# A two-layer diffusion transformer on one core: five of seven written-out instruction orders are replaced by orders from another search

## The chip, the cores and the metric

The kernel runs on one core of a Trainium2 chip. The metric is the time on the device, in microseconds (us), of one execution. The engines are TensorE (PE in the rows; PEld is its weight load), VectorE (DVE), ScalarE (ACT) and GpSimd (POOL); transfers between memory and the chip's SBUF are DMAs, most of them issued by SyncE (SP). Each engine works through its own queue in order.

## The reference, cut to what matters

The input is 512 latent tokens and 256 context tokens of width 1024, in float32. Layer 0 mixes tokens in two ways, by a long convolution ("Hyena") and by attention with 8 heads over 2 key heads, and layer 1 by a chunked matrix memory (mLSTM) in both directions. Around each mixer stand an adaptive norm, an output product, a second norm and a residual:

```python
        h_lat = rms_norm(x_lat, g_pre[layer]) * (1 + sc_l[:, None]) + sh_l[:, None]
        ...
            y_lat, y_ctx = even_mixer(h_lat, h_ctx, rows, cols, need_ctx, e_w_in[j], ...
            y_lat, y_ctx = odd_mixer(h_lat, h_ctx, need_ctx, o_w_in[j], ...
        x_lat = x_lat + ga_l[:, None] * rms_norm(y_lat, g_post[layer])
```

So between the layers each tile of 128 tokens goes through a chain: product with the output weights, norm of the product, gate, residual, norm for layer 1, scale and shift, and only then into the products of layer 1. After layer 1 only the 512 latent tokens are wanted.

## The kernel before

Every float32 product is made from values split in a high and a low part, by three matmuls (`mm3`, line 1015): high by high, high by low, low by high. Weights come in as `wr` by DMA, ScalarE copies the high part (`wh`) and VectorE subtracts to get the low part (`wl`); activations are split in the same way (`hTh`, `hTl`).

The program falls into seven regions, which follow each other: `start` (the norms and first products), `hy` (the long convolution), `att` (attention), `out0` (output product of layer 0, the norms between the layers and the first products of layer 1), `l1a` (layer 1's projections), `l1b` (its recurrence over 12 chunks of 64 tokens) and `out1` (its output product, norm and residual). In each region the code does not issue its operations at once. `record` (line 990) opens a list, every call on an engine is appended to it, and `play` (line 995) issues the whole list in the order of `ORDERS[name]`, a list of numbers: number i is the i-th operation that was recorded. All operations of a region are issued at line 1000, so all rows carry that line, and the names of the tiles tell operations apart. `tc.keep_in_program_order(x)` (line 1003) holds each engine's queue to that order. What an operation waits for across engines (data, a buffer that has to come free) is found from its operands and is not part of the order:

```python
        for i in ORDERS.get(name) or range(len(work)):
            e, fn, a, k = work[i].work
            x = fn(*a, **k)
```

A second table, `SLOTS`, says which of a tile's buffers the n-th allocation of a tag takes (`T`, line 930): "xn@9" is the tag `xn` in the tenth pool. A buffer is written again only when all readers of its previous tile are done. PSUM tiles are `pj` and `pm`, four buffers each in `out0`, `l1a` and `l1b`.

In `out0` the six tiles of tokens (4 and 5 are the context) go through these steps (`out_stages` from line 2074, `epi0`): the last product of the tile on PE (12 matmuls of 512 columns), `add` to `yacc` on VectorE, squares on ScalarE, reduce to `ess` and `esst` on VectorE, the power -1/2 `ers` on GpSimd (`rstd`, line 1076: one column of 128 values), the weighing by the gate `gg`, two multiply-adds into `xt` (residual), squares on ScalarE, `sst` on VectorE, the power `rs` on GpSimd, two `xn` on VectorE, eight transposes of `xn` on PE into `pm`, `hf` (scale and shift, shared by VectorE and ScalarE) and the split into `hTh` and `hTl`. Products of tiles that are ready with layer 1's first weights (288 columns) stand at the end of the region.

Of the kernel before, what the change touches and what calls it, by code (L numbers as in the profile page):

```python
# [151 lines left out]
class Ctx:  # L152
# [586 lines left out]
        0, 1, 2, 3, 4, 5,  # L739
    ],  # L740
    "sst@0": [
        0, 1, 4, 2, 3, 5,
    ],
    "rs@0": [
        0, 1, 2, 3, 4, 5,
# [150 lines left out]
        0, 1, 0, 1,  # L896
    ],
    "xt@15": [
        2, 0, 1, 3,
    ],  # L900
}

# [1875 lines left out]
```

## Time and profile before

| what | us |
|---|---|
| profiled execution, its time | 1491.61 |
| its span, from the first to the last instruction | 1489.8 |
| runs shown | 1490.02, 1491.35, 2872.85 |
| median of them | 1491.35 |
| PE busy in the span | 1457.7 (98%) |

The 1.8 us between span and time lie around the profiled instructions. The regions follow each other on PE with hardly an overlap; their borders by PE's first matmul are 0, 51.0, 423.6, 741.7, 878.4, 1043.9 and 1396.2 us, and the last matmul starts at 1481.44 us. TensorE's granted clock is given as a share of 2.4 GHz; its mean here is 0.997.

### The profile page before, as it was taken

The numbers are of one execution on the slowest core, as the hardware profiler recorded it, in microseconds if no ns is written. First come the engines' busy times: TensorE is split into PE (matmuls) and PEld (weight loads), VectorE is DVE, ScalarE is ACT, GpSimd is POOL, SyncE is SP. The second block draws the span as 40 slices with busy tenths as digits, with TensorE's granted clock in tenths as the row PEclk, the third lists the DMA queues.
The fourth block names the chain that finished last, engine by engine and source line by source line (L and its number), as shares of the span: only waits on it lengthen the run. The fifth ranks groups of instructions, "written<-read, shape, count | busy, mean of one in ns | idle before, by whom it ended". The sixth has DMA issues, their size and how long they took to land. (4 is left out here: it accounts for less than half of the span.)

```text
span 1489.8 us, 25927 instructions
## 1 busy us (share of the span) xinstructions
PE 1457.7 (98%) x10362; PEld 1339.3 (90%) x10362; DVE 1037.1 (70%) x1927; ACT 766.3 (51%) x1577; POOL 82.5 (6%) x125
## 2 busy tenths in 40 slices
PE   7999999999999999999999989999999999999997
PEld 5889999989998998989997789999999999999986
DVE  6687777887865666668325888666777777877455
ACT  6634343434435444446332567645766676666442
POOL 1100000001010000000000100000100000100000
PEclk9999999999999999999999999999999999999999
DMA  9755565457331121233462334675433322324463
GB/s 378 221 140 144 146 162 131 147 140 183 76 100 43 54 96 54 82 117 114 164 222 68 134 123 155 203 267 198 156 117 97 113 62 86 124 88 140 153 205 123
DMA packets 57353, 205.79 MB, mean 138 GB/s; under 512 B 7003, under 2 KB 8539, under 8 KB 54448
## 3 DMA queue, kind: packets, MB, share of 16 engines
q1 hardware_dynamic: 50968, 181.85, 35.9%
q0 software_dynamic: 5392, 21.11, 7.4%
q8 instruction: 81, 1.33, 0.4%
q10 hardware_dynamic: 872, 1.18, 0.3%
q14 instruction: 40, 0.33, 0.1%
HBM read 182.06 MB, written 51.41 MB: 157 GB/s over the span
## 5 line engine op out<-in xcount | busy, mean ns | idle before, releaser
L1000 PE MATMUL pj<-wh,hTh 128*128 128x256 f32 (+2 forms) x1200 | 340.6, 290 | 0.8 <-ACT qjunk L1000 0.4
L1000 PE MATMUL pj<-wl,hTh 128*128 128x256 f32 (+2 forms) x1200 | 337.4, 287 | 0.3 <-DVE wl L1000 0.3
L1000 PE MATMUL pj<-wh,hTl 128*128 128x256 f32 (+2 forms) x1200 | 336.7, 288 | 0.0
L1000 PE MATMUL pj<-hTh,wh 128*128 128x512 f32 (+1 forms) x832 | 286.8, 346 | 0.4 <-DVE vl L1000 0.3
L1000 PE MATMUL pj<-hTl,wh 128*128 128x512 f32 (+1 forms) x832 | 285.4, 344 | 0.4 <-DVE hTl L1000 0.4
L1000 PE MATMUL pj<-hTh,wl 128*128 128x512 f32 (+1 forms) x832 | 285.5, 345 | 0.0
L1000 PEld LDWEIGHTS pj<-wh,hTh 128*128 128x128 f32 x1200 | 224.3, 189 | 6.2 <-issue 2.7
L1000 PEld LDWEIGHTS pj<-wl,hTh 128*128 128x128 f32 x1200 | 225.0, 189 | 2.9 <-DVE wl L1000 0.5
L1000 PEld LDWEIGHTS pj<-wh,hTl 128*128 128x128 f32 x1200 | 223.9, 189 | 3.5 <-issue 1.5
L1000 DVE TENSOR_TENSOR wl<-wr,wh 128x1024 fp32r<-128x1024 f32 (+1 forms) x142 | 171.4, 1213 | 63.9 <-ACT wh L1000 63.9
L1000 ACT CAST wh<-wr 128x1024 fp32r<-128x1024 f32 (+1 forms) x142 | 146.7, 1043 | 83.4 <-PE pj L1000 55.8
L1000 PEld LDWEIGHTS pj<-hTh,wh 128*128 128x128 f32 x832 | 156.6, 189 | 18.5 <-DVE vl L1000 1.1
L1000 PEld LDWEIGHTS pj<-hTl,wh 128*128 128x128 f32 x832 | 156.8, 189 | 17.9 <-DVE hTl L1000 0.7
L1000 PEld LDWEIGHTS pj<-hTh,wl 128*128 128x128 f32 x832 | 156.4, 188 | 18.0 <-DVE wl L1000 0.3
L1000 DVE TENSOR_TENSOR PTl<-pj,PTh 128x384 fp32r<-128x384 f32 (+1 forms) x80 | 41.1, 526 | 18.8 <-ACT PTh L1000 18.4
L1000 ACT CAST PTh<-pj 128x384 fp32r<-128x384 f32 (+1 forms) x80 | 35.6, 459 | 30.5 <-PE pj L1000 29.8
L1000 DVE TENSOR_TENSOR wl<-ch,wh 128x1024 fp32r<-128x1024 f32 x28 | 34.2, 1221 | 24.5 <-ACT wh L1000 24.4
L1000 DVE TENSOR_REDUCE mx<-s 128x1 f32<-128x768 f32 (+1 forms) x48 | 37.2, 775 | 11.4 <-PE s L1000 11.2
L1000 PE MATMUL pm<-Rh,dfa 128*128 128x256 f32 (+1 forms) x192 | 45.0, 305 | 0.0
L1000 DVE TENSOR_TENSOR med<-big 128x512 f32<-128x512 f32 (+1 forms) x48 | 40.4, 864 | 5.0 <-ACT big L1000 4.8
L1000 PE MATMUL s<-dfa,qTh 128*128 128x256 f32 (+1 forms) x160 | 42.8, 338 | 0.7 <-ACT hdh L1000 0.6
L1000 DVE SCALAR_TENSOR_TENSOR C<-C,apb,pj 128x258 f32<-128x258 f32 x64 | 30.8, 481 | 16.5 <-PE pj L1000 11.8
(374 smaller groups left out, 3172.1 us busy)
## 6 DMA issues: line engine op xcount, KB each, us to landing
wr<-in_e_w_in SPq DMA_DIRECT2D x52, 512.0 KB, 5.3
wr<-in_o_w_in SPq DMA_DIRECT2D x50, 512.0 KB, 5.2
o_sums<-in_o_w_in POOLq DMA_DIRECT2D x28, 512.0 KB, 7.1
ch<-o_sums SPq DMA_DIRECT2D x21, 512.0 KB, 4.9
wh<-in_w_mod SPq DMA_DIRECT2D x10, 1024.0 KB, 7.3
wl<-in_w_mod SPq DMA_DIRECT2D x9, 1024.0 KB, 7.6
wr<-in_e_w_out SPq DMA_DIRECT2D x16, 512.0 KB, 4.5
wr<-in_o_w_out SPq DMA_DIRECT2D x16, 512.0 KB, 4.6
```

What stands on the lines that cost most here:

```text
L1000: x = fn(*a, **k)
```

## The change

The body of the program is the same, and no instruction is added or removed. Replaced are the lists of numbers in `ORDERS` for `att`, `out0`, `l1a`, `l1b` and `out1` (those for `start` and `hy` stay), and the buffer numbers in `SLOTS` that go with them. The operations of `start` and `hy` keep their buffers, some under another number. An operation's place in the list moves by 26 (att), 32 (out0), 11 (l1a), 22 (l1b) and 32 (out1) places on the mean, by some hundreds at most. The orders come from a search that works with assumed durations, here with longer ones for GpSimd's small operations and for landings of transfers; neither the search nor its durations are part of the program.

The core of the diff, where the last tiles of `out0` go through their norms, and two of the buffer tables:

```diff
@@ -304,514 +304,514 @@
...
-        665, 666, 664, 663, 667, 682, 643, 670, 671, 672, 676, 675, 674, 677, 683, 684, 644, 646, 645, 685, 756, 686, 687, 688, 689, 668, 690, 691,
-        728, 729, 730, 692, 731, 708, 709, 678, 718, 719, 720, 721, 725, 710, 711, 712, 713, 714, 715, 716, 717, 738, 735, 694, 724, 722, 695, 693,
-        739, 740, 732, 741, 742, 743, 744, 745, 746, 747, 748, 749, 734, 733, 696, 765, 766, 767, 699, 698, 723, 726, 727, 750, 768, 769, 770, 771,
-        772, 736, 701, 702, 751, 737, 773, 774, 753, 754, 775, 703, 705, 787, 788, 704, 791, 752, 792, 755, 757, 777, 778, 776, 779, 782, 780, 929,
-        783, 784, 781, 758, 789, 790, 785, 794, 700, 815, 760, 793, 786, 761, 797, 798, 799, 800, 801, 802, 803, 804, 805, 806, 807, 808, 824, 825,
-        826, 827, 828, 829, 830, 831, 832, 795, 833, 834, 835, 856, 762, 809, 857, 858, 859, 860, 861, 862, 863, 796, 810, 763, 812, 927, 836, 837,
-        838, 839, 924, 813, 932, 764, 811, 814, 817, 816, 864, 865, 928, 866, 867, 843, 846, 819, 842, 840, 820, 821, 868, 847, 848, 849, 925, 956,
-        822, 883, 933, 957, 884, 885, 934, 935, 936, 937, 938, 852, 759, 823, 869, 871, 930, 872, 980, 886, 981, 873, 853, 841, 870, 844, 874, 875,
-        876, 818, 850, 851, 854, 931, 845, 878, 879, 855, 890, 939, 940, 880, 889, 888, 882, 958, 959, 960, 961, 893, 894, 895, 896, 962, 963, 964,
-        965, 966, 967, 898, 900, 968, 969, 887, 970, 971, 972, 973, 897, 941, 942, 943, 944, 945, 946, 913, 947, 899, 948, 914, 915, 949, 974, 975,
-        976, 881, 903, 904, 905, 877, 891, 892, 982, 901, 906, 902, 983, 984, 985, 986, 987, 988, 909, 916, 918, 907, 910, 917, 919, 950, 951, 952,
...
+        665, 643, 666, 681, 682, 683, 684, 685, 686, 687, 688, 663, 689, 690, 691, 671, 672, 676, 697, 674, 706, 692, 707, 708, 709, 710, 711, 644,
+        646, 712, 713, 714, 715, 716, 717, 738, 739, 740, 694, 695, 667, 696, 675, 645, 673, 677, 693, 699, 698, 701, 728, 729, 730, 731, 678, 741,
+        668, 742, 743, 744, 732, 734, 735, 733, 745, 746, 747, 748, 749, 750, 702, 751, 718, 719, 720, 723, 765, 724, 721, 766, 767, 722, 725, 726,
+        768, 769, 770, 771, 772, 773, 774, 775, 776, 797, 798, 736, 703, 799, 800, 753, 801, 754, 752, 756, 923, 700, 705, 824, 704, 815, 755, 757,
+        758, 760, 802, 803, 804, 787, 727, 759, 788, 789, 737, 777, 793, 761, 762, 781, 790, 778, 779, 780, 783, 784, 791, 805, 806, 807, 794, 808,
+        825, 826, 827, 828, 829, 830, 782, 831, 832, 833, 834, 835, 809, 792, 785, 763, 836, 837, 810, 786, 812, 813, 764, 795, 796, 811, 841, 846,
+        847, 848, 814, 816, 849, 817, 927, 924, 850, 852, 928, 856, 857, 858, 859, 860, 861, 862, 863, 864, 865, 819, 820, 866, 956, 867, 840, 868,
+        930, 853, 838, 839, 842, 925, 957, 958, 843, 821, 823, 893, 932, 869, 871, 872, 931, 822, 873, 844, 874, 875, 851, 870, 876, 854, 845, 878,
+        855, 879, 959, 894, 895, 960, 961, 933, 934, 935, 962, 963, 964, 965, 966, 896, 899, 898, 897, 900, 883, 967, 968, 969, 970, 884, 885, 886,
+        889, 890, 901, 936, 937, 980, 981, 877, 887, 971, 972, 938, 888, 973, 974, 939, 940, 941, 942, 943, 891, 880, 881, 882, 902, 944, 945, 946,
+        892, 903, 904, 905, 906, 910, 908, 913, 907, 917, 914, 909, 915, 916, 947, 920, 948, 949, 950, 951, 918, 975, 976, 919, 952, 953, 954, 982,
...
     "yraw@9": [
-        1, 1, 0, 0, 0, 1, 1, 1,
+        1, 1, 1, 0, 0, 1, 0, 1,
     ],
...
     "xn@9": [
-        1, 0, 1, 2, 2, 0, 1, 2, 0, 1, 0, 2,
+        1, 0, 1, 2, 2, 0, 1, 0, 0, 2, 1, 2,
     ],
...
```

Numbers of `out0` that matter here: the last matmul of the last product is 690 for tile 0, 749 for tile 1, 808 for tile 2, 867 for tile 3. The transposes are 718 to 721 and 728 to 731 (tile 5), 777 to 780 and 787 to 790 (tile 0), 836 to 839 and 846 to 849 (tile 1), 883 to 886 and 893 to 896 (tile 2), 903 to 906 and 913 to 916 (tile 3). On VectorE 809 and 868 are the `add` of tiles 2 and 3, 812, 813 and 871, 872 the reduces and `esst`, 811 and 870 the weighing, 816, 817 and 875, 876 the multiply-adds, 820 and 879 `sst`, 822, 823 and 881, 882 the `xn`; 763 and 764 are the `xn` of tile 1; 925, 928 and 931 are the low parts `wl` of layer 1's first weights. On GpSimd 703, 762, 821 and 880 are the powers `rs` of tiles 0 to 3, 814 and 873 the powers `ers` of tiles 2 and 3.

## Rows read from the trace of the kernel before

**Rows 1.** The page: busy us and share of the span, by engine.

```profile
PE 1457.7 (98%) x10362; PEld 1339.3 (90%) x10362; DVE 1037.1 (70%) x1927; ACT 766.3 (51%) x1577; POOL 82.5 (6%) x125
```

**Rows 2.** Windows by region: us; PE, PEld, DVE, ACT, POOL busy; PEclk; DMA; GB/s.

```profile
0.00:423.60 423.60, 412.69 (x2696) 368.93 (x2697) 327.47 (x542) 190.53 (x306) 32.07 (x52) 1.00 0.59 166
423.60:741.70 318.10, 314.14 (x2414) 292.10 (x2412) 201.59 (x480) 148.12 (x383) 14.37 (x9) 1.00 0.27 93
741.70:878.40 136.70, 130.57 (x794) 111.33 (x794) 81.43 (x143) 60.63 (x116) 8.94 (x15) 0.99 0.42 144
878.40:1043.90 165.50, 164.79 (x1321) 161.98 (x1322) 120.37 (x160) 100.70 (x138) 0.00 (x0) 1.00 0.58 192
1043.90:1396.20 352.30, 349.86 (x2596) 331.91 (x2595) 265.29 (x546) 238.10 (x584) 24.90 (x45) 1.00 0.33 106
1396.20:1489.80 93.60, 85.64 (x550) 73.06 (x548) 40.91 (x59) 28.27 (x53) 2.22 (x4) 0.98 0.52 182
```

**Rows 3.** PE's waits in att, first of seven lines: us in total, times, longest.

```profile
PE pj L1000 <- ACT qjunk L1000: 0.9, 3, 0.4
...
```

**Rows 4.** PE's waits in out0, all of them.

```profile
PE pm L1000 <- DVE xn L1000: 4.0, 5, 1.0
PE pm L1000 <- ACT hf L1000: 0.6, 1, 0.6
PE pj L1000 <- DVE wl L1000: 0.3, 1, 0.3
```

**Rows 5.** PE's waits in l1a, all of them.

```profile
PE pm L1000 <- DVE wa L1000: 1.3, 1, 1.3
PE pj L1000 <- DVE cvo L1000: 0.7, 1, 0.7
```

**Rows 6.** PE's waits in l1b, all of them; out1 has none.

```profile
PE pj L1000 <- DVE vl L1000: 2.1, 4, 1.1
PE pm L1000 <- DVE hh L1000: 0.2, 1, 0.2
```

**Rows 7.** Tile rs on GpSimd: shortest, median, longest ns; first and last start.

```profile
L1000 POOL TENSOR_TENSOR rs<-sst,mhalf x12: 549/562/1074, 5.8 to 863.4; 128x1 f32<-128x1 f32 x12
```

**Rows 8.** PE's timeline, tile 0 of out0: start, us, [idle before, releaser].

```profile
835.01 0.40 PE L1000 MATMUL pj<-wl,yoh 128*128 128x512 f32 x1
835.24 0.40 PE L1000 MATMUL pj<-wh,yol 128*128 128x512 f32 x1
835.90 0.66 PE L1000 MATMUL pm<-c_ident,xn 128*128 128x128 f32 x4 [0.27 <-DVE xn L1000]
...
845.56 0.81 PE L1000 MATMUL pm<-c_ident,xn 128*128 128x128 f32 x4 [0.90 <-DVE xn L1000]
```

**Rows 9.** Windows, tiles 2 and 3 of out0.

```profile
850.00:860.00 10.00, 9.03 (x51) 7.55 (x49) 9.51 (x24) 7.12 (x15) 2.31 (x4) 1.00 0.41 153
...
867.60:871.10 3.50, 3.50 (x16) 3.48 (x17) 1.40 (x3) 0.68 (x3) 0.23 (x3) 0.51 1.01 410
```

**Rows 10.** VectorE's timeline, from tile 2's add to tile 3's xn.

```profile
850.66 0.68 DVE L1000 TENSOR_TENSOR yacc<-pj,yacc 128x512 f32<-128x512 f32 x1
...
864.61 0.48 DVE L1000 TENSOR_SCALAR xn<-xt,rs 128x512 f32<-128x512 f32 x1
```

**Rows 11.** PE's timeline, matmuls of 288 columns.

```profile
863.81 0.30 PE L1000 MATMUL pj<-wh,hTh 128*128 128x288 f32 x1
863.94 0.29 PE L1000 MATMUL pj<-wl,hTh 128*128 128x288 f32 x1
```

**Rows 12.** VectorE's timeline, before l1a's first transpose.

```profile
877.65 0.42 DVE L1000 TENSOR_TENSOR vl<-pj,vh 128x256 fp32r<-128x256 f32 x1
877.98 0.28 DVE L1000 TENSOR_TENSOR wa<-pj,gb 128x128 f32<-128x128 f32 x1
```

**Rows 13.** VectorE's timeline, the end of out1.

```profile
1483.41 0.69 DVE L1000 TENSOR_TENSOR yacc<-yacc,gg 128x512 f32<-128x512 f32 x1 [0.85 <-ACT junk L1000]
...
1485.09 1.41 DVE L1000 SCALAR_TENSOR_TENSOR xt<-yacc,ers,xt 128x512 f32<-128x512 f32 x2 [0.73 <-POOL ers L1000]
```

More of the change, by code (lines that the diff above doesn't have):

```diff
@@ L729 @@
     "xt@0": [
-        1, 4, 3, 5, 0, 2, 4, 1, 3, 5, 2, 4,
+        3, 5, 4, 0, 2, 1, 5, 3, 4, 0, 1, 5,
     ],
     "wr@1": [
[4 rows of a table removed]
[4 rows of a table added]
     ],
@@ L741 @@
     "sst@0": [
-        0, 1, 4, 2, 3, 5,
+        0, 1, 2, 3, 4, 5,
     ],
     "rs@0": [
-        0, 1, 2, 3, 4, 5,
+        0, 1, 4, 3, 2, 5,
     ],
     "pj@2": [
-        0, 1, 0, 1, 2, 3, 0, 2, 1, 3, 2, 0, 1, 3, 2, 0, 1, 3, 3, 0, 1, 2, 0, 3, 1, 1, 3, 1, 0, 2, 3, 1, 0, 2, 0, 1, 3, 2, 0, 1, 2, 3, 1, 3, 2, 0, 1,
-        3, 2, 0, 3, 1, 2, 0, 3, 1, 0, 2, 3, 1, 0, 2, 2, 1, 0, 3, 2, 1, 0, 0, 3, 2,
+        0, 3, 0, 3, 1, 2, 0, 1, 3, 2, 1, 0, 3, 2, 1, 0, 3, 2, 2, 0, 3, 1, 0, 2, 3, 3, 2, 3, 0, 1, 2, 3, 0, 1, 0, 3, 2, 1, 0, 3, 1, 2, 3, 2, 1, 0, 3,
+        2, 1, 0, 2, 3, 1, 0, 2, 3, 0, 1, 2, 3, 0, 1, 1, 3, 0, 2, 1, 3, 0, 0, 2, 1,
     ],
@@ L754 @@
     "pm@3": [
[4 rows of a table removed]
[4 rows of a table added]
     ],
     "g@4": [
-        0, 1, 0, 1, 0, 1, 0, 1,
+        1, 0, 1, 0, 1, 0, 1, 0,
     ],
     "x0s@4": [
-        0, 1, 0, 1, 0, 1, 0, 1,
+        1, 0, 1, 0, 1, 0, 1, 0,
     ],
@@ L769 @@
     "med@4": [
[3 rows of a table removed]
[3 rows of a table added]
     ],
     "big@4": [
-        0, 1, 0, 0, 1, 0, 0, 1, 0, 0, 1, 0, 0, 1, 0, 0, 1, 0, 0, 1, 0, 0, 1, 0,
+        1, 0, 1, 1, 0, 1, 1, 0, 1, 1, 0, 1, 1, 0, 1, 1, 0, 1, 1, 0, 1, 1, 0, 1,
     ],
     "rt@6": [
-        1, 0, 0, 1, 0, 1, 0, 0, 1, 1, 0, 1, 1, 0, 1, 0, 1, 1, 0, 1, 0, 1,
+        0, 1, 1, 1, 1, 1, 0, 0, 1, 0, 1, 0, 1, 0, 1, 0, 0, 1, 0, 1, 0, 1,
     ],
     "gs@6": [
-        0, 0, 1, 2, 0, 1, 2, 0, 1,
+        0, 0, 2, 1, 0, 2, 1, 0, 2,
     ],
     "qTl@6": [
-        0, 1, 0, 2, 1, 0, 2, 1, 0,
+        0, 2, 0, 1, 2, 0, 1, 2, 0,
     ],
     "qTh@6": [
-        0, 0, 1, 2, 0, 1, 2, 0, 1,
+        0, 0, 2, 1, 0, 2, 1, 0, 2,
     ],
@@ L802 @@
     "rq@6": [
-        2, 3, 0, 1, 2,
+        1, 2, 3, 0, 1,
     ],
     "s2@8": [
-        1, 0, 1, 0, 0, 1, 1, 0, 0, 1, 0, 1, 1, 1, 0, 1, 0, 1, 1, 0, 1, 0, 1, 1, 0, 1, 0, 1, 1, 0, 0, 1, 0, 0, 1, 1, 0, 0, 1, 0, 1, 0, 0, 1, 1, 0, 1,
-        0,
+        0, 1, 1, 0, 1, 0, 0, 1, 0, 1, 1, 0, 0, 0, 1, 0, 1, 0, 0, 1, 0, 1, 1, 0, 0, 1, 0, 1, 0, 0, 1, 1, 0, 1, 0, 0, 1, 0, 1, 0, 1, 0, 0, 1, 0, 1, 0,
+        1,
     ],
     "mx@6": [
-        3, 2, 0, 1, 2, 3, 1, 0, 2, 3, 0, 1, 2, 3, 0, 2, 1, 3, 0, 2, 1, 3, 0, 2, 1, 3, 0, 2, 3, 1, 0, 2, 1, 0, 3, 1, 2, 3, 0, 2, 1, 3, 2, 0, 1, 3, 0,
-        2,
+        2, 1, 0, 3, 1, 2, 0, 3, 2, 1, 0, 3, 2, 1, 0, 2, 3, 1, 0, 2, 3, 1, 0, 2, 1, 3, 0, 2, 1, 3, 0, 1, 2, 3, 0, 1, 2, 3, 0, 1, 2, 3, 0, 1, 2, 0, 3,
+        1,
     ],
     "sm@6": [
-        3, 2, 1, 0, 2, 3, 0, 1, 2, 3, 1, 0, 3, 2, 1, 0, 3, 2, 1, 0, 3, 2, 1, 0, 3, 2, 1, 0, 2, 3, 1, 0, 3, 1, 2, 3, 0, 1, 2, 0, 3, 1, 0, 2, 1, 3, 0,
+        1, 0, 3, 2, 0, 1, 2, 3, 0, 1, 3, 2, 0, 1, 3, 2, 0, 1, 3, 2, 1, 0, 3, 2, 1, 0, 3, 2, 1, 0, 3, 2, 1, 0, 3, 2, 1, 0, 3, 2, 1, 0, 3, 2, 1, 0, 3,
         2,
@@ L862 @@
     "cvo@12": [
-        0, 1, 2, 0, 1, 2, 0, 1, 2, 0, 1, 2, 0, 1, 2, 0, 1, 2,
+        0, 2, 1, 0, 2, 1, 0, 2, 1, 0, 2, 1, 0, 2, 1, 2, 0, 1,
     ],
@@ L868 @@
     "decay@14": [
-        0, 1, 0, 1, 1, 0, 0, 1, 1, 0, 1, 0, 0, 1, 1, 0,
+        0, 1, 0, 1, 0, 1, 1, 0, 0, 1, 1, 0, 0, 1, 1, 0,
     ],
     "C@14": [
-        0, 1, 0, 1, 0, 1, 0, 1, 0, 1, 0, 1, 0, 1, 0, 0, 1, 0, 1, 0, 1, 0, 1, 0, 1, 1, 0, 1, 0, 1, 1, 0, 1, 0, 1, 0, 1, 0, 1, 0, 1, 0, 1, 0, 1, 1, 0,
-        1, 0, 1, 1, 0, 1, 0, 1, 0, 1, 0, 1, 0, 1, 0, 1, 0, 1, 1, 0, 1, 0, 1, 0, 1, 0, 1, 0, 0, 1, 0, 1, 0,
+        1, 0, 1, 0, 1, 0, 1, 0, 1, 0, 1, 0, 1, 0, 1, 1, 0, 1, 0, 1, 0, 1, 0, 1, 0, 0, 1, 0, 1, 0, 0, 1, 0, 1, 0, 1, 0, 1, 0, 1, 0, 1, 0, 1, 0, 0, 1,
+        0, 1, 0, 0, 1, 0, 1, 0, 1, 0, 1, 0, 1, 0, 1, 0, 1, 0, 1, 0, 1, 0, 1, 0, 1, 0, 1, 0, 0, 1, 0, 1, 0,
     ],
     "Ch@14": [
-        0, 1, 0, 1, 0, 1, 1, 0, 0, 1, 1, 0, 0, 1, 0, 1, 0, 1, 0, 1, 1, 0, 1, 0, 1, 0, 1, 0, 1, 0, 1, 0, 0, 1, 1, 0, 1, 0, 1, 0, 1, 0, 1, 0, 1, 0, 1,
-        1, 1, 0, 1, 0, 1, 0, 1, 0, 1, 0, 0, 1, 1, 0, 1, 0,
+        1, 0, 1, 1, 0, 1, 0, 1, 1, 0, 1, 0, 0, 1, 0, 1, 1, 0, 1, 0, 1, 0, 1, 0, 0, 1, 0, 1, 0, 1, 0, 1, 0, 1, 0, 1, 0, 1, 0, 1, 1, 1, 0, 1, 0, 1, 0,
+        0, 1, 0, 0, 1, 0, 1, 0, 1, 0, 1, 1, 0, 1, 0, 1, 0,
     ],
     "Cl@14": [
-        0, 1, 0, 1, 0, 1, 0, 1, 1, 0, 1, 0, 0, 1, 0, 1, 0, 1, 1, 0, 0, 1, 1, 0, 1, 0, 1, 0, 1, 0, 1, 0, 0, 1, 0, 1, 0, 1, 1, 0, 1, 0, 1, 0, 1, 1, 0,
-        0, 1, 0, 1, 0, 1, 0, 1, 0, 1, 0, 0, 1, 1, 0, 1, 0,
+        1, 0, 1, 1, 0, 1, 0, 1, 1, 0, 0, 1, 1, 0, 1, 0, 0, 1, 0, 1, 0, 1, 1, 0, 0, 1, 0, 1, 0, 1, 0, 1, 0, 1, 1, 0, 1, 0, 0, 1, 1, 1, 0, 1, 0, 1, 0,
+        0, 1, 0, 0, 1, 0, 1, 0, 1, 0, 1, 1, 0, 1, 0, 1, 0,
     ],
     "dn@14": [
-        1, 0, 0, 2, 3, 2, 2, 1, 1, 0, 0, 3, 3, 2, 2, 1,
+        0, 1, 2, 1, 1, 3, 3, 0, 0, 2, 2, 1, 1, 3, 3, 0,
     ],
     "yraw2@15": [
-        0, 1, 2, 3, 0, 1, 2, 3,
+        0, 1, 3, 0, 1, 0, 2, 2,
     ],
@@ L898 @@
     "xt@15": [
-        2, 0, 1, 3,
+        0, 2, 1, 3,
     ],
```

852 rows, old and new, of tables (ORDERS, SLOTS) are left out of this document.

## The prediction

> **What bounds the kernel.** Four views were read. The page first: PE is busy 1457.7 of 1489.8 us, VectorE 1037.1, and GpSimd, whose assumed durations are what differed in the search, 82.5 [rows 1]. The windows by region then say where PE's missing 32 us lie: 10.9 in start and hy, 4.0 in att, 6.1 in out0, 0.7 in l1a, 2.4 in l1b and 8.0 in out1 [rows 2]. Third, the waits of PE in each region from att on name who ends the idle time: in att nine short ones, 3.9 us by seven lines of which the first is shown [rows 3]; in out0 `xn`, the normed tile that is transposed, with 4.0 us in five waits, and 0.9 for `hf` and `wl` [rows 4]; in l1a two [rows 5]; in l1b five [rows 6]; in out1 none. In all these lists no wait of PE on a transfer or on GpSimd itself appears. GpSimd's powers and the landings act at most through a VectorE step behind them. Last, the timelines around each wait, in which PE's order and VectorE's order can be laid beside the new lists.
>
> So the kernel is bound by PE's own work, and an order can only move the idle time. What is left after 423.6 us is 21.2 us of idle time [rows 2], 8.4 of it the tail behind the last matmul at 1481.44, and one stretch of 3.5 us at a granted clock of 0.51, the 1.2 GHz level, right behind the waits of tiles 2 and 3 [rows 9]; at the 2.4 GHz level its work would take 0.51 x 3.5 = 1.8, so it costs 1.7. Even if all of that went, the time would fall by 23 us, 1.5%.
>
> **The change part by part.** No instruction comes or goes; each term below is a wait that grows or shrinks. start and hy keep order and buffers but for names: 0.
>
> *A, tiles 5 and 0 in out0.* After the last product of tile 0 (matmul starting at 835.24, ending 835.64), PE waits 0.27 for tile 5's `xn`, then 0.90 for tile 0's [rows 8], then 0.55 for a PSUM buffer that `hf` frees (the 0.6 of [rows 4]): 1.7 in all. The chain from that product to tile 0's `xn` took 835.64 to 845.56 = 9.9 us. Before, PE has 33 matmuls of 512 columns and 8 transposes to fill it; at 0.23 each (835.01 to 835.24, [rows 8]) and some 0.15 per transpose (0.66 for four) that is 8.8. In the new list 45 matmuls and 10 transposes stand there: 45 x 0.23 + 10 x 0.15 = 11.8, over 9.9. Tile 5's transposes move behind some 3 us more of products, and the transposes of tile 0 are spread between products, which gives `hf` time. All three waits go: -1.7 (bounds -1.7 and +1, should the chain, which now has tile 5's splits in its VectorE queue, lengthen by 3 us).
>
> *B, tiles 2 and 3.* The remaining `xn` waits are 4.0 - 0.27 - 0.90 = 2.8, and with `wl` 3.1 [rows 4]; the slow clock behind them costs 1.7. In this stretch VectorE is the busier engine: 9.51 of 10 us from 850 to 860, PE 9.03 [rows 9]. From the `add` of tile 2 (809) to the first `xn` of tile 3 (882) it ran from 850.66 to 865.09 = 14.4 us [rows 10]; the durations of its operations add up to 16.3, since neighbours overlap (factor 0.885). PE's work between tile 2's last product and tile 3's first transposes was 24 matmuls of 512 columns, 35 of 288 (0.13 apart, [rows 11]) and 16 transposes, 12.2 us. That is a gap of 2.2, and the second `xn` (881), which came later, cost another 1.0, the longest wait of [rows 4]: 3.2 by the sum, 3.1 measured. In the new list 881 and 882 stand side by side, and PE's part is 23, 36 and 16, 12.1 us; VectorE's part up to the first `xn`, with one more long `wl` and the splits placed ahead of tile 3's steps, adds up to 17.8 us, by 0.885 15.8. The gap is 15.8 - 12.1 = 3.7: +0.5, and the clock stays as it is. Bounds: -4.8 if VectorE finds its way through without a gap (3.1 and 1.7 gone), +2.5 if nothing overlaps. I take the value near the measured factor, as this stretch's own rows gave it.
>
> First what a row shows: the same power of one column took 549 ns at its shortest, 562 in the median and 1074 at its longest [rows 7]. The Trainium skill (GPSIMD Engine Reference, 1. Specifications) says that GpSimd shares its SBUF interface with VectorE and contends with VectorE instructions that have two SBUF inputs; the spread of that row agrees with it, though no row shows the cause. By that rule one longer duration for all powers would be wrong both for those beside such operations and for the others, and the two powers of a tile's chain at their longest would give back 2 x 0.5 = 1.0 of the sum's gain.
>
> *C, l1a's start.* PE's first transpose waits 1.28 (the 1.3 of [rows 5]) for `wa`. In the new list PE has 8.9 us of work behind tile 3's transposes, 7.9 before, by the same pitches; VectorE has one more `vl` ahead of `wa`, 0.33 from start to start [rows 12]. -1.0 + 0.3 = -0.7 (bounds -1.3 and +0.4).
>
> *D, the convolution in l1a.* 0.7 for `cvo` [rows 5]. Before, the product that needs it stands directly behind; in the new list 1.3 us of other products lie between: -0.7 (bounds -0.7 and 0).
>
> *E, l1b.* Five waits, 2.3 us [rows 6]. At four of the five the new list puts 0.5 to 2.9 us more PE work between the step that releases and the matmul that waits, which alone would take about 2. Against that: I counted the matmuls that stand directly behind the VectorE or ScalarE step they need, with no PE work between (zero lead). They rise from 18 to 31. Each such place waits only if the engine in front runs late. I take -0.5, bounds -2.3 and +1.7.
>
> *F, att.* 3.9 us in nine waits [rows 3]. Zero-lead places rise from 34 to 44: fewer at the transposes of probabilities (12 to 7), more at PSUM buffers and scores. +0.5, bounds -3.9 and +3.
>
> *G, out1.* No wait before, so nothing to gain in the body. In the tail the new list puts tile 2's two multiply-adds (1.41) ahead of tile 3's reduce; they fill the 0.85 of waiting for ScalarE's squares, and the weighing of 0.69 moves under the power, a wait of 0.73 [rows 13]: 0 (bounds -0.5 and +1.5).
>
> Sum: -1.7 + 0.5 - 0.7 - 0.7 - 0.5 + 0.5 = -2.6. From the profiled 1491.6 that is 1489.0; the median of the runs is 0.3 lower, so 1488.7.
>
> SyncE's loads are reordered with everything else. As no wait of PE on a landing stands in the lists, their order is costed at 0; if a weight load came late it would show as a wait on `wh` or `wl`, where only 0.3 stands in out0 [rows 4] today.
>
> **The rivals.** *Slower: waits move to the zero-lead places.* In att and l1b 23 such places are new. The waits there now are 3.9/9 = 0.43 and 2.3/5 = 0.46 us long [rows 3, 6]. If all 23 waited, they would cost 10; half of them 5; it overtakes the gain of 2.6 from about 6 on. For it: the new lists leave less slack in the two regions with the most operations. Against: 52 such places exist now and only 14 waits. It gives 1493.7 to 1498. Chance 0.20.
>
> *Larger gain: VectorE keeps up at tiles 2 and 3.* Then B is -4.8 in place of +0.5, and the time 1483.5 or so (1482 to 1486.5). For it: the splits are spread differently, and the factor 0.885 can be lower in an order with more neighbours of the same kind. Against: VectorE has more to do there than before. Chance 0.18. On what the clock does: its fall came right behind the last of these waits [rows 9]. The Trainium skill (TensorE: Matmul & The Clock Gate, Part 1: The HAM clock gate) ties the lower clock to idle stretches of PE; that agrees with the row, and by it the 1.7 us goes only when the waits go, not with a part of them.
>
> *Nothing: what A gains, tile 2 gives back.* VectorE bounds the whole stretch from 845 to 867, so PE that comes through tile 0 without waiting arrives 1.7 us earlier at tile 2 and waits there. Then out0 yields nothing, and C to F about -1 with an uncertainty as large: 1490.3 to 1492.6. For it: 9.51 of 10 [rows 9]. Against: VectorE's chain starts with PE's product, which also comes earlier. Chance 0.22.
>
> **How the numbers follow.** The forecast (1486.5 to 1490.3) has 0.40, the rivals 0.20, 0.18 and 0.22. The likeliest is the forecast, 1488.7. The range 1484 to 1495 leaves out half of the larger gain and the upper half of the slower case, 0.17 or so. The 2% that a measurement of this kernel can tell from no change are 30 us. A gain of that size is beyond the 23 us that there are to gain: 0.01. A loss of it would take a load so late that PE stalls for tens of microseconds: 0.02. Within 2%: 0.97.
>
> **What would show it.** Right: PE's waits in out0 no longer hold the ones at tiles 5 and 0; those at tiles 2 and 3 are still there with 3 us or more and a stretch at half the clock behind them; l1a's wait on `wa` is 0.6 or less and that on `cvo` is gone; the sums in att and l1b lie within 1 us of 4 and 2; out1 has none and its tail is again 8.4 us. Wrong: att or l1b with 15 or more waits (the slower rival); no stretch at half the clock in out0 (the larger gain); any wait of PE on a `wh` or `wl` behind a landing in l1a or out1, which I have costed at nothing.

## The result, and the profile after

The changed kernel took 1497.06 us in the median of five runs, before 1491.35; the ratio is 1.0049, interval 1.0033 to 1.0065. It is slower by 5.7 us, where 1488.7 and a range up to 1495 had been forecast. Its profiled execution took 1496.96 us with a span of 1495.2.

The page's first part, engines and busy time, tells little: PE is busy 3.6 us longer than in [rows 1], with the same 10362 matmuls.

```profile
PE 1461.3 (98%) x10362; PEld 1344.5 (90%) x10362; DVE 1036.7 (69%) x1927; ACT 764.3 (51%) x1577; POOL 82.1 (5%) x125
```

The windows by region, with the borders at PE's first matmul of each and the columns of [rows 2]:

```profile
0.00:423.10 423.10, 412.79 (x2696) 369.03 (x2697) 327.41 (x542) 190.41 (x306) 32.00 (x52) 1.00 0.59 166
423.10:741.40 318.30, 314.33 (x2415) 293.35 (x2413) 201.68 (x479) 147.42 (x383) 14.42 (x9) 1.00 0.27 93
741.40:886.40 145.00, 134.77 (x793) 114.99 (x793) 83.60 (x148) 60.16 (x116) 8.68 (x15) 0.95 0.38 132
886.40:1051.10 164.70, 164.70 (x1322) 161.86 (x1321) 117.66 (x156) 99.75 (x137) 0.00 (x0) 1.00 0.57 196
1051.10:1401.75 350.65, 349.35 (x2596) 332.12 (x2595) 266.83 (x546) 239.04 (x586) 23.87 (x45) 1.00 0.33 107
1401.75:1495.20 93.45, 85.33 (x550) 73.19 (x548) 39.49 (x58) 27.57 (x53) 3.12 (x4) 0.98 0.52 184
```

Against [rows 2] the whole loss is in out0: 145.0 for 136.7 us. att is 0.2 us longer, start and hy 0.5 shorter, l1a is 0.8 and l1b 1.65 us shorter, out1 0.15. In out0 two things grew: PE's idle time, from 6.1 to 10.2 us, and its busy time, from 130.6 to 134.8; its mean clock is 0.95. PE's waits in out0, all of them, name the first; those before are [rows 4]:

```profile
PE pm L1000 <- ACT hf L1000: 3.4, 2, 2.9
PE pm L1000 <- DVE hf L1000: 3.4, 1, 3.4
PE pj L1000 <- DVE wl L1000: 1.4, 1, 1.4
PE pm L1000 <- DVE xn L1000: 1.1, 1, 1.1
PE pj L1000 <- ACT yacc L1000: 0.4, 1, 0.4
PE pm L1000 <- DVE sst L1000: 0.4, 1, 0.4
PE pm L1000 <- DVE ess L1000: 0.2, 1, 0.2
```

The `xn` waits that I had worked on fell from 4.0 to 1.1. In their place stand 6.8 us of waits of a transpose on `hf`, a step that comes behind the transposes. PE's timeline of out0 shows where:

```profile
845.49 0.33 PE L1000 MATMUL pm<-c_ident,xn 128*128 128x128 f32 x1 [3.37 <-DVE hf L1000]
852.85 0.70 PE L1000 MATMUL pm<-c_ident,xn 128*128 128x128 f32 x4 [0.40 <-DVE sst L1000]
861.39 0.44 PE L1000 MATMUL pm<-c_ident,xn 128*128 128x128 f32 x2 [0.56 <-ACT hf L1000]
863.21 0.40 PE L1000 MATMUL pj<-wl,hTh 128*128 128x288 f32 x1 [1.39 <-DVE wl L1000]
...
872.02 0.79 PE L1000 MATMUL pm<-c_ident,xn 128*128 128x128 f32 x5 [1.05 <-DVE xn L1000]
875.66 0.90 PE L1000 MATMUL pm<-c_ident,xn 128*128 128x128 f32 x3 [2.86 <-ACT hf L1000]
```

The first, second, third and last of these lines are the transposes 721 (tile 5), 790 (tile 0; the profile names `sst`, which stands directly behind the `hf` step in question), 838 (tile 1) and 914 (tile 3). Four transposes fill the four quarters of one PSUM tile `pm`, and four `hf` steps read them. In the new order 721 stands behind 723 and 724, which read other quarters of the same tile, and the program makes a write into a PSUM tile wait for the readers issued before it, whichever quarter they read: the 3.37 us end with a `hf` of another quarter. I call these late writes. The old order has six (670 to 672, 780, 789, 790) in three tiles, of which one place waits (0.55); the new order has ten (721, 778 to 780, 790, 838, 839, 914 to 916) in five tiles, and four places wait, 3.37 + 0.40 + 0.56 + 2.86 = 7.2 us. By the list, each of these four stands directly behind the `hf` step that it waits for, with no work of PE between.

VectorE's timeline and then ScalarE's show why the first of these readers was so late:

```profile
842.50 0.73 DVE L1000 TENSOR_SCALAR hf<-pm,scl,shf 128x128 f32<-128x128 f32 x2 [0.61 <-ACT hf L1000]
...
843.74 0.14 DVE L1000 TENSOR_SCALAR sst<-ss 128x1 f32<-128x1 f32 x1
845.02 0.41 DVE L1000 TENSOR_SCALAR hf<-pm,scl,shf 128x128 f32<-128x128 f32 x1 [1.14 <-ACT hf L1000]
```

```profile
840.72 1.06 ACT L1000 ACTIVATE junk<-xt 128x1024 bf16<-128x1024 f32 x1 [1.38 <-DVE xt L1000]
...
843.26 0.46 ACT L1000 ACTIVATE hf<-pm,shf,scl 128x128 f32<-128x128 f32 x1 [0.80 <-DVE hf L1000]
843.92 0.63 ACT L1000 ACTIVATE junk<-yacc 128x512 f32<-128x512 f32 x1 [0.20 <-DVE sst L1000]
...
844.54 0.44 ACT L1000 ACTIVATE hf<-pm,shf,scl 128x128 f32<-128x128 f32 x1
```

ScalarE's `hf` stands behind the squares of tiles 0 and 1, each `hf` of VectorE waits for the one of ScalarE before it, and PE waits for the last at 845.02. The second thing that grew, PE's busy time, is read from windows behind the waits:

```profile
845.00:850.50 5.50, 5.01 (x16) 3.97 (x17) 4.53 (x11) 2.34 (x4) 0.89 (x1) 0.69 0.16 39
...
863.50:867.20 3.70, 3.51 (x16) 3.27 (x16) 3.56 (x8) 1.60 (x3) 1.42 (x1) 0.56 0.02 4
...
875.60:881.00 5.40, 5.33 (x23) 5.34 (x24) 3.81 (x7) 2.25 (x6) 0.00 (x0) 0.50 0.44 178
```

Three stretches are wholly or partly at the 1.2 GHz level, where [rows 9] has one. I price each at its busy time times one less its clock: 5.01 x 0.31 + 3.51 x 0.44 + 5.33 x 0.50 = 5.8 us, against 1.7.

So the account closes over out0 and l1a together, 2113 matmul records in both kernels. The windows of this stretch, before and after:

```profile
741.75:1043.85 302.10, 295.27 (x2113) 273.21 (x2114) 201.80 (x302) 161.28 (x253) 8.94 (x15) 0.99 0.51 170
```

```profile
741.38:1051.09 309.71, 299.48 (x2113) 276.85 (x2114) 201.26 (x303) 159.91 (x252) 8.68 (x15) 0.98 0.48 166
```

7.6 us longer: 3.4 of idle time (6.83 to 10.23) and 4.2 of the same work at the lower clock. l1b gives 1.7 back. What brings the lower clock is not shown by this one execution.

### The profile page after: what moved, and what is told of

It is laid out like the page before. It is cut to its first block, busy times and chain, and to the rows that moved or that the text cites. A ratio compares the mean times of both kernels' runs of the same rounds, so it can differ in the third digit from the quotient of the medians.

```text
span 1495.2 us, 25901 instructions
## 1 busy us (share of the span) xinstructions
PE 1461.3 (98%) x10362; PEld 1344.5 (90%) x10362; DVE 1036.7 (69%) x1927; ACT 764.3 (51%) x1577; POOL 82.1 (5%) x125
## 5 line engine op out<-in xcount | busy, mean ns | idle before, releaser
L1000 ACT ACTIVATE qjunk<-pj 128x128 f32<-128x128 f32 x60 | 16.6, 277 | 55.3 <-PE pj L1000 23.4
```

## The experiments

The theory after the result: the loss is in out0, from late writes and the half clock behind them. The rival: VectorE's chain from tile to tile bounds that stretch, and a wait of PE that is taken away at one tile comes back at the next. Two runs first place the loss. Beside each run stand runs of the kernel before on the same chip (medians 1490.52 to 1491.23 us); the ratios are against these, so they compare better than the times.

**The old out0 in the new kernel.** Its buffers go with it.

```diff
     "out0": [
-        51, 53, 361, 362, 55, 54, 56, 60, 59, 57, 58, 52, 1, 77, 78, 79, 80,
+        51, 53, 56, 54, 52, 55, 60, 57, 58, 59, 63, 64, 61, 62, 68, 66, 65,
...
```

> The changed kernel with the order and buffers of out0 alone taken back. If the loss lies in out0 alone (on PE it lasts 145.0 us there against 136.7 before), the new orders of att, l1a, l1b and out1 keep their gains (l1a and l1b are 0.8 and 1.6 us shorter between their borders): 1487 to 1489 us, with out0 at 135 to 137 us. If the shorter l1a and l1b are only a gift of the longer out0 before them (loads that landed during its waits), they grow back: 1490.5 to 1492.

1490.13 us, ratio 0.9993 (0.9983 to 1.0002). In the profile out0 and l1a last 302.86 us, l1b 350.5. The time lies between the two that were expected. The loss is gone with out0, and l1b keeps its gain; l1a does not: its wait on `wa` is back with 1.6 us. That gain had come with the late PE of the new out0.

**The new out0 alone**, the same edit the other way in the kernel before.

> The kernel before with only the order and buffers of out0 replaced by the new ones. Loss in out0 alone: out0 lasts 144 to 146 us, the whole 1498.5 to 1501, slower than the full change. If it takes the new attention or layer-1 orders as well: 1491 to 1494.

1500.16, ratio 1.0059 (1.0044 to 1.0074): 8.9 us over before (1491.23 on this chip), more than the whole change and as expected. out0 and l1a: 311.51 us, of which PE is busy 300.22.

**The late writes first.** Ten transposes are moved ahead of the first read of their tile; each line moves the first number behind the second.

```diff
+for _r, _i, _j in (
+    ("out0", 721, 720),
+    ("out0", 778, 777),
+    ("out0", 779, 778),
+    ("out0", 780, 779),
+    ("out0", 790, 780),
+    ("out0", 838, 837),
+    ("out0", 839, 838),
+    ("out0", 914, 913),
+    ("out0", 915, 914),
+    ("out0", 916, 915),
+):
+    ORDERS[_r].remove(_i)
+    ORDERS[_r].insert(ORDERS[_r].index(_j) + 1, _i)
```

> The changed kernel, in which ten transposes (721, 778 to 780, 790, 838, 839, 914 to 916 of out0) that stand behind a read of the PSUM tile they write are moved ahead of that read. Theory of the late writes: PE waits there for the reader, 3.37 + 0.40 + 0.56 + 2.86 = 7.2 us, and 3 to 4 us of half clock follow; both go: 1486 to 1488. Rival, VectorE's queue is late whatever PE's order is: the waits come back at the next consumer, xn or hTl, and the time stays within 2 us of 1497.

1493.14, ratio 1.0014 (1.0005 to 1.0023), between the two. PE's waits in out0 and l1a now:

```profile
PE pm L1016 <- DVE xn L1016: 3.0, 3, 1.3
PE pj L1016 <- DVE wl L1016: 2.3, 1, 2.3
PE pm L1016 <- DVE wa L1016: 1.9, 1, 1.9
PE pm L1016 <- ACT hTh L1016: 0.9, 1, 0.9
PE pj L1016 <- ACT yacc L1016: 0.4, 1, 0.4
```

No wait on `hf` is left, but 8.5 us of others: idle time fell only from 10.2 to 8.6 us, busy time from 299.5 to 296.8 (of 305.39). Both theories hold a part: most of the waiting moved on to other steps, VectorE's above all, and 2.7 us of half clock went. Of the 7.6 us that out0 and l1a had lost, 4.3 are back; 3.3 are left with no late write in the list.

**Tile 3's late writes alone** (the last three lines of the list).

> The same for the three transposes of tile 3 alone (914 to 916). Late writes with the clock: the wait of 2.86 goes and the 5.4 us at half clock behind it give 2.7: 1491 to 1492. Late writes, but the half clock has another cause: 1494. VectorE's queue late anyway: 1496 to 1498.

1495.52, ratio 1.0029 (1.0017 to 1.0040), off all three expectations. The wait of 2.86 went, and the one on tile 3's `xn` ahead of it grew from 1.05 to 2.6. The runs of this one kernel fall into two groups: three with a mean clock of 0.997 took 1493.1 to 1493.5, four with 0.994 to 0.995 took 1495.5 to 1498.0. The profiled execution is of the first group: 721 waits 3.38 us as in the changed kernel, and so do 838 and the product behind it (0.56 and 1.38), but the clock is full from 864 to 870, where the second slow stretch lies, and in the windows behind 721:

```profile
843.00:847.00 4.00, 0.88 (x6) 0.47 (x4) 2.26 (x7) 2.62 (x7) 0.55 (x1) 1.00 0.51 202
847.00:852.50 5.50, 5.25 (x25) 4.25 (x25) 4.55 (x11) 2.58 (x5) 0.89 (x1) 1.00 0.21 51
```

Up to tile 3 the two kernels have the same order. So the same idle time brings the lower clock in one execution and not in another. At the full clock PE reaches tile 3 earlier, and that is why it waits longer for `xn` there. In this execution out0 and l1a last 304.93 us, 4.8 less than in the changed kernel, and 4.0 of that is PE's busy time (295.47): the group at 0.997 is as fast as the kernel without any late write.

**Tile 5's late write alone** (721, the first line).

> The changed kernel with the one transpose 721 of tile 5 moved ahead of the reads of its tile, nothing else. Late writes: the wait of 3.37 goes and the half clock after it, and tile 0's own chain shows as a wait of about 1 in its place; those at tiles 0 to 3 and their clock stay: 1492.5 to 1494.5. Rival: the stretch behind is bound by VectorE, so the whole 3.4 comes back by tile 1: 1496 to 1497.5.

1496.49, ratio 1.0036 (1.0024 to 1.0048): the rival's number. PE's timeline:

```profile
848.51 0.70 PE L1007 MATMUL pm<-c_ident,xn 128*128 128x128 f32 x4 [0.90 <-DVE xn L1007]
851.86 1.12 PE L1007 MATMUL pm<-c_ident,xn 128*128 128x128 f32 x4 [2.65 <-DVE sst L1007]
```

The 3.37 of 721 are gone, 0.90 appears at tile 0's `xn`, and the late write 790 behind it waits 2.65 where it had waited 0.40: 3.55 for 3.77. Tile 0's chain is late in any case. But the 2.65 is a late write again: 790 stands behind 793, a `hf` far back in VectorE's queue. So this run shows that the wait comes back, and not which of the two theories is right.

**VectorE without its waits on ScalarE.** The ten moves, and tile 5's `hf` steps of ScalarE ahead of the squares.

```diff
+    ("out0", 733, 732),
+    ("out0", 701, 733),
+    ("out0", 723, 721),
+    ("out0", 722, 723),
+    ("out0", 751, 722),
```

> The changed kernel with the ten transposes first, and in addition the steps hf of tile 5 put together by engine: ScalarE's four (732, 733, 723, 722) stand ahead of the squares of tile 0 (701) and of tile 1 (751) that held them up, so that VectorE's hf steps need not wait for them. Theory: the loss that was left is VectorE waiting for ScalarE in the alternating hf steps (0.61 + 1.14 + 0.53 = 2.3 us between 843 and 848); then the wait of 0.9 on tile 0's xn goes, and a part of the later ones (0.9 hTh, 2.3 wl, 1.9 wa): 1489.5 to 1491.5. Rival: VectorE's own load (one more wl ahead of tile 3's chain) sets the later waits: tile 0's wait goes, those from 853 on grow by as much, 1492.5 to 1494.

1492.62, ratio 1.0008 (0.9998 to 1.0018). Tile 0's wait is gone as expected; out0 and l1a last 305.32 us against 305.39, with 1.4 us less idle time and 1.4 more at the lower clock. The time is the rival's number, but not by the rival's way: the later waits did not grow (7.2 us are left of 8.5), and what was gained at tile 0 went to the clock in this execution. Its mean clock was 0.995; of the ten runs the six at 0.995 took 1492.5 to 1494.0, the four at 0.997 took 1489.5 to 1492.5.

**The same test on the old order.** The old out0 in the new kernel, its six late writes first (670 to 672, 780, 789, 790).

> The old order of out0 with the new ones of att, l1a, l1b and out1, and the six transposes of the old order that stand behind a read of their own PSUM tile (670 to 672, 780, 789, 790) moved ahead of it. Theory of the late writes: the wait of 0.55 on hf at tile 0 goes, the rest stays: 1489 to 1490, 0.5 under the mix without the moves. Rival: the wait moves to the next xn: 1490 again, with the same sum of waits in out0.

1490.51, ratio 0.9996 (0.9987 to 1.0006). The wait of 0.55 is gone, and tile 2's, 0.99 in the mix without the moves, is 1.70:

```profile
860.43 0.33 PE L1012 MATMUL pm<-c_ident,xn 128*128 128x128 f32 x1 [1.70 <-DVE xn L1012]
```

That is the rival's case: the wait moved to the next `xn`.

**Busy in place of idle.** The changed kernel; the line in `play` issues a matmul of tile 2 thirteen times more.

```diff
             e, fn, a, k = work[i].work
+            for _ in range(13 if (name, i) == ("out0", 765) else 0):
+                tc.keep_in_program_order(fn(*a, **{**k, "stop": True}))
             x = fn(*a, **k)
```

> The changed kernel with 13 extra copies of a matmul of tile 2 (765, started anew each time, so that its result is the same), 13 x 0.23 = 3.0 us of PE work ahead of the transpose 721 that waits 3.37 us. PE is busy there in place of idle, nothing else is earlier. If the idle time brings the half clock: the stretch at 845 to 850.5 (5.01 us of PE work at 0.69, a loss of 1.5) is at the full clock, and the time falls by 1.5 although PE does more work: 1495 to 1496. If the half clock has another cause or only the work counts: 1497 to 1498.

1496.63, ratio 1.0038 (1.0026 to 1.0051), between the two expectations; its interval and that of the changed kernel overlap. The clock is clearer: it is 0.996 or 0.997 in all five runs, 0.993 or 0.994 in all five of the changed kernel. In the profile 721 waits 0.35, and two of the three slow stretches are gone; the waits ahead of tile 3:

```profile
862.41 0.40 PE L1002 MATMUL pj<-wl,hTh 128*128 128x288 f32 x1 [1.38 <-DVE wl L1002]
...
871.22 0.79 PE L1002 MATMUL pm<-c_ident,xn 128*128 128x128 f32 x5 [2.60 <-DVE xn L1002]
```

```profile
846.00:851.00 5.00, 4.93 (x23) 4.00 (x24) 4.05 (x11) 2.25 (x4) 0.89 (x1) 1.00 0.17 41
862.50:867.50 5.00, 4.81 (x36) 4.58 (x37) 4.86 (x10) 2.00 (x4) 1.42 (x1) 1.00 0.00 0
872.00:880.00 8.00, 5.14 (x26) 5.13 (x26) 5.17 (x10) 3.75 (x9) 0.00 (x0) 0.57 0.63 231
```

Over out0 and l1a the time fell by 1.8 us (307.95 for 309.71) with 13 x 0.23 = 3.0 us more work. The wait of 1.38 that stood ahead of the second slow stretch is still there, with the full clock behind it, so that wait alone does not bring the lower one. And a part of what the clock gave came back as idle time: PE waits 2.60 us for tile 3's `xn`, 1.05 in the changed kernel. As the runs with one and the same wait differ in their clock, this supports the idle time as the cause and doesn't prove it.

**Can the mix be made faster?** Four edits in the old out0 with the new other regions: VectorE's three long sums behind the first `wa` of l1a; this and tile 3's `xn` steps together; the latter alone; and the latter with all first `vl` and `wa` ahead of the sums. In the lines below the first three are the first edit and the fourth is in the other three edits; the last three are of the fourth edit, in which 72 and 74 follow 73 as in the first.

```diff
+    ("l1a", 73, 11),
+    ("l1a", 72, 73),
+    ("l1a", 74, 72),
...
+    ("out0", 881, 882),
...
+    ("l1a", 8, 11),
+    ("l1a", 7, 8),
+    ("l1a", 73, 7),
```

> The old order of out0 with the new ones of the other regions, and in l1a VectorE's three long sums for the convolution (73, 72, 74; 1.22 us each) moved behind the first steps vl and wa of the gates, which PE's first transpose of l1a waits for. Theory: those 1.6 us of waiting come from VectorE's queue alone and the sums have slack: the wait on wa goes and nothing takes its place, 1488.5 to 1489, with l1a 1.6 us shorter. Rival: the sums are then late for the convolution's products, and a wait on cvo or d1h of 1 us or more appears: 1490.

> As the kernel with wa before the long sums, and in the old order of out0 the second xn of tile 3 (881) behind the first (882), ahead of four hf steps. Theory: PE's second wait of 1.0 at tile 3 goes, and the half clock behind the two waits may go with it (1.7): 1487.5 to 1488.5 without, 1486 to 1487 with it. Rival: VectorE bounds the stretch, so hf is later by the same time and the wait turns up on hTl or on wa: 1488.5 to 1489.5.

> The old order of out0 with the new ones of the other regions, and only the second xn of tile 3 (881) moved behind the first (882). In the kernel that had this and the moved sums, out0 was 2.7 us shorter with no half clock, and 3.0 us of waits on wa and vl stood in l1a. Theory: those waits belong to the move of the sums, so here one wait on wa of 1.6 to 2.6 is left: out0 and l1a together 300.5 to 301.5 us, the whole 1488 to 1489.5. Rival: VectorE's load comes back on wa whatever its order: out0 and l1a together 302 to 303, 1490 to 1491.

> The same, and in l1a the first gate steps of all three products (vl 10, 13, 7 and wa 14, 11, 8) ahead of the three long sums. Theory: VectorE's order at the border is the cause of the waits on wa, and with all of them first none is over 0.5: out0 and l1a together 299 to 300.5 us, the whole 1486.5 to 1488.5. Rival: VectorE's load bounds the border and the waits only change their names: 301.5 to 303, 1489.5 to 1491.

| kernel | us | ratio, interval | out0 + l1a | PE busy there | idle |
|---|---|---|---|---|---|
| sums behind `wa` | 1491.40 | 1.0002 (0.9993 to 1.0011) | 304.14 | 296.31 | 7.83 |
| this and `xn` together | 1490.65 | 0.9998 (0.9989 to 1.0007) | 302.25 | 294.56 | 7.69 |
| `xn` together alone | 1490.41 | 0.9999 (0.9990 to 1.0008) | 302.38 | 295.32 | 7.06 |
| all `vl`, `wa` first | 1491.80 | 1.0006 (0.9997 to 1.0015) | 303.49 | 295.31 | 8.18 |
| old out0, no moves | 1490.13 | 0.9993 (0.9983 to 1.0002) | 302.86 | 295.61 | 7.25 |

No time is the one that the theory gave. The third lies in its rival's range; the other three lie above both, and the wait on `cvo` or `d1h` that the first edit's rival expected did not come: PE waits 1.6 us for `wa` in three pieces and 0.6 for `vl`. With `xn` together the second wait at tile 3 is gone, and the wait on `wa` is 2.5 us in the one without the moved sums, against 1.6; with all `vl` and `wa` first it is 3.3 in two. Something else went: with `xn` together one of the two waits ahead of the slow stretch of [rows 9] is left, 0.84 and 0.87 us in the second and third edit, and the stretch is at the full clock (in the third a lower one, 0.79, came behind the wait on `wa`). In the second:

```profile
865.00:873.00 8.00, 6.84 (x51) 6.41 (x51) 6.46 (x15) 4.80 (x12) 1.06 (x4) 1.00 0.95 310
```

No edit brought the idle time of this stretch under 7 us, and no version is shown to beat the kernel before.

## Why the prediction was wrong

The step that failed is A, with a term that the sum does not have. A let all waits around tile 0 go; in their place came four late writes with 7.2 us of waiting, so that PE's idle time grew by 3.4 us in sum, and 4.2 us more of work at the lower clock. Putting the transposes first gave back 4.3 of the 7.6 us. The 3.3 that are left point to a longer way through VectorE from tile to tile, which A and B had mis-sized.

**What bounds the kernel.** Right as to PE and as to the stretch that VectorE bounds. It was said there that out0's tiles 2 and 3 are VectorE's; waits that were taken away at tile 5, at tile 0 of the old order, at tile 3 and at l1a's first gates all came back further on as waits, wholly or in part, so the whole way from tile 0 to these gates seems to be.

**A failed first.** It kept the 9.9 us from tile 0's last product to its `xn` and gave PE 11.8 us of work; all waits were to go. With 721 out of the way, the chain took from 836.05 (the product's last matmul starts at 835.66 and lasts 0.39) to 848.51 = 12.5 us. VectorE's timeline in the kernel before and then in that kernel, in which the reader adds the waits for ScalarE:

```profile
840.23 0.41 DVE L1000 TENSOR_SCALAR hf<-pm,scl,shf 128x128 f32<-128x128 f32 x1 [0.30 <-ACT hf L1000]
...
842.16 0.69 DVE L1000 TENSOR_TENSOR hTl<-hf,hTh 128x512 fp32r<-128x512 f32 x1 [0.21 <-ACT hTh L1000]
...
843.73 0.15 DVE L1000 TENSOR_SCALAR sst<-ss 128x1 f32<-128x1 f32 x1 [0.28 <-ACT junk L1000]
```

```profile
838.26 0.15 DVE L1007 TENSOR_REDUCE ess<-ss 128x1 f32<-128x2 f32 x1 [0.74 <-ACT junk L1007]
...
843.24 0.73 DVE L1007 TENSOR_SCALAR hf<-pm,scl,shf 128x128 f32<-128x128 f32 x2 [0.61 <-ACT hf L1007]
...
845.77 0.41 DVE L1007 TENSOR_SCALAR hf<-pm,scl,shf 128x128 f32<-128x128 f32 x1 [1.14 <-ACT hf L1007]
846.71 0.41 DVE L1007 TENSOR_SCALAR hf<-pm,scl,shf 128x128 f32<-128x128 f32 x1 [0.53 <-ACT hf L1007]
```

That is 0.8 us of waiting for ScalarE before and 3.0 now, most of the 2.6 by which the chain grew. Tile 5's four `hf` of VectorE stood in this chain in the old list too. Moving tile 5's transposes back, which was to free PE, put the last two of them (724, 725) between tile 0's `sst` and its `xn`, behind ScalarE's squares of tiles 0 and 1. The bound of +1 allowed for a chain 3 us longer, and I took the other end; but it named the wrong steps, as tile 5's splits (727, 737) stand ahead of tile 0's `xn` in the old list and behind it in the new one. The sentence "the transposes of tile 0 are spread between products, which gives `hf` time" had it the wrong way round: the 0.55 was no wait for a free buffer but a late write, and spreading transposes between `hf` steps makes more of them. Nothing in the working looked at what a write into a PSUM tile waits for.

**B failed in its size and in the clock.** From tile 2's add at 854.63 to tile 3's `xn` (PE goes on at 872.02) the chain took 17.4 us, predicted 15.8, [rows 10] 14.4. The sum of 17.8 was right, though not by one more `wl`: both lists have the same three there, and the new one has a split (786) and two `hf` of tile 2 (899, 900) more. The overlap of 0.885 did not hold, as VectorE waits for ScalarE in two places, 0.26 and 0.94 us. The wait on tile 3's `xn` is only 1.05, as PE itself came late, but the late write 914 adds 2.86, and the clock did not stay as it was: 5.8 us for 1.7. That the 1.7 goes only when all the waits go did not hold in the second and third edit of the mix: one of the two waits was left, and the clock behind it was full.

**C was right for another reason, D right.** The waits on `wa` and `cvo` are gone. D is in the order of l1a: 0.7 us of `cvo` stay with the new out0 alone. C goes with a late PE and comes back, 1.9 us, when the late writes are taken away.

**E was mis-sized.** l1b is 1.7 us shorter, not 0.5; three waits of 1.2 us in sum are left of [rows 6]. **F:** att is 0.2 us longer, for +0.5. **G was right:** no wait in out1, a tail of 8.5 us for 8.4.

**The rivals.** The time fell in the range of the slower rival, but not by its mechanism: neither att nor l1b has more waits. Zero-lead places were the right kind of suspect in the wrong regions: the four late writes that wait are such places, and the count did not separate those that only wait for data from those that also write into a tile being read. The third rival, that tile 2 gives back what tile 0 gains, is what the runs of 721 alone and of the old order with its late writes first showed.

**Open.** Which waits bring the lower clock in which execution, and so how much of the 4.3 us that the transposes first gave back is theirs and how much the clock's: the execution with only tile 3's moved lost 4.8 us less, nearly all by its clock. And what makes up the 2.5 us by which the stretch stays longer without late writes (305.4 against 302.9). Between tile 0's `add` and its `xn` the new list has two `hf` and a split of tile 4, tile 5's two `xn` and tile 1's weighing more, and tile 5's two splits less: no run moved them alone.

## What to carry to other kernels

When an order is changed by hand or by a search, list for every buffer that several steps fill and read in parts which writes stand behind a read of the same buffer: each can be a wait (four of ten were here) that a model of durations alone does not have. In a stretch that a second engine bounds, a wait of PE taken away at one place can come back at the next (3.55 of 3.77 us at tile 5), so it is the length of that engine's chain, its waits on third engines included, that has to be summed for both orders, not PE's room. Price the clock with the waits: here the same matmuls took 4.2 us more behind 3.4 us more of idle time.

## What the runs showed of the hardware

In this program a late write and an `hf` that alternates between ScalarE and VectorE can both wait: 3.37 and 2.86 us for PE at the longest, 0.26 to 1.14 for VectorE each time. The Trainium skill (PSUM — Partial Sum Buffer, PSUM bank collisions raise a hardware error) says that two engines may not access one bank in the same partitions at once, reads against reads included, and that the compiler back end's scheduler adds a dependency between such instructions, "ACT↔DVE too, not just a PE write against a reader". The waits above agree with it. By that rule four transposes and four reads of one tile run one after the other wherever they alternate.

GpSimd's power on one column took 1.42 us at 864.27, the longest of one column in either kernel; it ran beside VectorE's subtraction of `wl`, 1.22 us long, which the new order puts right behind `esst`, where the power starts. VectorE's timeline with the multiply-add `xt` that needs the power, then GpSimd's:

```profile
864.04 1.22 DVE L1000 TENSOR_TENSOR wl<-wr,wh 128x1024 fp32r<-128x1024 f32 x1
865.17 0.48 DVE L1000 TENSOR_SCALAR xn<-xt,rs 128x512 f32<-128x512 f32 x1
865.73 0.75 DVE L1000 SCALAR_TENSOR_TENSOR xt<-yacc,ers,xt 128x512 f32<-128x512 f32 x1
```

```profile
861.73 0.55 POOL L1000 TENSOR_TENSOR rs<-sst,mhalf 128x1 f32<-128x1 f32 x1 [4.13 <-DVE sst L1000]
864.27 1.42 POOL L1000 TENSOR_TENSOR ers<-esst,mhalf 128x1 f32<-128x1 f32 x1 [1.99 <-DVE esst L1000]
```

The power took 0.9 us longer than the 0.55 ahead of it. That agrees with the contention that the prediction had weighed, but no run parts the power from its neighbour. It cost little: VectorE was busy with `wl` and `xn` to 865.65, and `xt` starts 0.08 us later, where VectorE's neighbours overlap by 0.1 elsewhere. So the chain lost 0.2 us at most, of the 1.0 that the prediction had thought possible.
